# Down-projection in seven block products, with its left operands prepared in the up stage

## Chip, cores and metric

One core of one Trainium2 chip. The metric is the device time of one execution in microseconds, for the slowest core; here there is only one. All arithmetic is float32 at the interface; inside, each matmul operand is split into a high part (float32r) and a low remainder, and each product is three matmuls: high by high, high by low, low by high.

## The reference

One decoder layer of 1024 tokens and width 1024: a mixer (a state-space scan beside sparse attention), a LayerNorm, then the feed-forward part, then a second LayerNorm. The change lies in the feed-forward part and what follows it:

```
def _conv_ffn(h, w_up, conv_w, conv_b, w_down):
    u = _causal_dwconv(h @ w_up, conv_w, conv_b)
    gate, up = jnp.split(u, 2, axis=-1)
    return (jax.nn.silu(gate) * up) @ w_down
...
        h = _layer_norm(DEEPNORM_ALPHA * x + m, ln1_g[i], ln1_b[i])
        f = _conv_ffn(h, ffn_w_up[i], ffn_conv_w[i], ffn_conv_b[i], ffn_w_down[i])
        x = _layer_norm(DEEPNORM_ALPHA * h + f, ln2_g[i], ln2_b[i])
```

`w_up` is 1024 x 5632, the convolution has width 3 along the tokens, `w_down` is 2816 x 1024.

## The kernel before

The framework orders each engine's instructions by a priority list against a simulated clock, and gives out buffers from pools with fixed counts; only SyncE, which issues the loads, keeps the order of the program. Every engine then runs its list in order, so an instruction that waits holds those behind it.

**Up stage** (the loop over `j`, 22 tiles of 128 channels). For each `j`, two raw weight tiles are loaded (`up_load`), and `w_prep` forms four combinations on VectorE (lines 988 to 991), then seven operand pairs: a high copy on ScalarE (line 996) and a low remainder on GpSimd (line 997). TensorE runs seven block products (`product`, 12 matmuls each, 84 in all) in place of eight. They accumulate in PSUM banks `pa`, `pb`, `pc`, `pd`; VectorE and ScalarE combine them into `xg` and `xu` (lines 1023 to 1047). A bank is read between the two products that accumulate on it: `c1` must be copied out of `pa` (line 1023) while the next product runs on `pb`. Then comes the convolution: one ScalarE pass with scale and bias (line 1052) from SBUF to SBUF, two VectorE passes for the other taps (line 1055), for `xu` and `xg`, each 1024 wide; SiLU (line 1056), the product of the two (line 1057), and one store of 512 KB to DRAM (`g_dr`, line 1058), issued from ScalarE's queue.

**Down stage** (two halves of 512 tokens). For each half all eight PSUM banks accumulate, over 22 tiles `k` of the inner dimension. `prep(k)` loads a row tile of `w_down` (512 KB) and the half of `g_dr` (256 KB), and splits both: `w_hi` on ScalarE (line 129), `w_lo` on GpSimd (line 130), `g_hl` on ScalarE and VectorE (lines 1074 and 1075). `down(k, b)` is six matmuls. For the last three or four `k` of a half (`TAILS`) the loop over token tiles is outermost, so that the residual sum (line 1102) and `layer_norm` (lines 223, 224, 755, 756, 765, 766) of one token tile run beside the matmuls of the next.

All matmuls go through `three` (lines 157 to 159).

Of the kernel before, what the change touches and what calls it, by code (L numbers as in the profile page):

```python
# [15 lines left out]
P = 128  # L16
# [41 lines left out]
def hybrid_layer(ctx, tc, x, w_in, ssd_conv_w, ssd_conv_b, dt_bias, a_log, d_skip, ssd_norm_g,  # L58
# [14 lines left out]
    BUFS = {"wr": 3, "wh": 3, "wl": 3, "t4": 18, "wo": 8, "pp": 8, "pt": 3, "tx": 3}  # L73
# [48 lines left out]
    g_dr = dram.tile([DFF, L], F32, name="g_dr")  # L122
# [895 lines left out]
    def first(j, w):  # L1018

        a = bank("pa", "ip")  # L1020
        product(a, w[0], h11, True)
        c1 = mid("c1")
        nc.scalar.activation(c1, a, AF.Copy)
        return a, c1

    for j in range(NF):
        up_load(j + 1)
        w = ws.pop(j)
        a, c1 = first(j, w)
# [102 lines left out]
```

## Time and profile before

| | us |
|---|---|
| median of 3 runs | 1746.84 (1745.46 to 1746.99) |
| the profiled execution | 1747.83 |
| its span, first to last instruction | 1745.8 |
| up stage, dense part | 1075 to 1486.5 |
| TensorE idle between the stages | 1486.5 to 1494.4 |
| down stage | 1494.4 to 1736.8 |
| after the last matmul | 1736.8 to 1745.8 |

The profile is of one execution. A matmul's own duration overlaps with its neighbours', so its price in a dense stretch is the distance from one start to the next. A group's duration of VectorE or GpSimd includes the time in which the instruction was held by the other engine. The granted clock is a share of 2.4 GHz.

### The profile page before, as it was taken

The numbers are of one execution on the slowest core, as the hardware profiler recorded it, in microseconds if no ns is written. First come the engines' busy times: TensorE is split into PE (matmuls) and PEld (weight loads), VectorE is DVE, ScalarE is ACT, GpSimd is POOL, SyncE is SP. The second block draws the span as 40 slices with busy tenths as digits, with TensorE's granted clock in tenths as the row PEclk, the third lists the DMA queues.
The fourth block names the chain that finished last, engine by engine and source line by source line (L and its number), as shares of the span: only waits on it lengthen the run. The fifth ranks groups of instructions, "written<-read, shape, count | busy, mean of one in ns | idle before, by whom it ended". The sixth has DMA issues, their size and how long they took to land.

```text
span 1745.8 us, 22765 instructions
## 1 busy us (share of the span) xinstructions
PE 1624.8 (93%) x7976; PEld 1346.9 (77%) x7976; DVE 1192.9 (68%) x2089; ACT 889.3 (51%) x1625; POOL 801.3 (46%) x560
## 2 busy tenths in 40 slices
PE   7899998998998699999999977999999999899997
PEld 5688887776897568777787755888888888688886
DVE  3533779999368477787777478887887786515516
ACT  3333597687632476666666344544444443333231
POOL 2222234634265254545454348755555552445351
PEclk9999999999999889999999987999999999899999
DMA  5122022131333464454553551222222223446443
GB/s 168 38 79 67 27 92 88 43 115 52 125 103 91 151 202 127 127 167 118 162 147 124 171 169 60 85 94 76 77 84 93 85 73 115 139 145 229 157 153 125
DMA packets 180938, 198.22 MB, mean 114 GB/s; under 512 B 12003, under 2 KB 136279, under 8 KB 180823
## 3 DMA queue, kind: packets, MB, share of 16 engines
q1 hardware_dynamic: 147351, 145.37, 28.1%
q10 hardware_dynamic: 33472, 51.39, 8.1%
q8 instruction: 63, 1.03, 0.3%
q14 instruction: 52, 0.43, 0.1%
HBM read 145.28 MB, written 51.45 MB: 113 GB/s over the span
## 4 chain that ended last, share of the span: by engine, by line
PE 50%; DVE 8%; issue 2%; ACT 2%; DMA 2%; POOL 0%; ACTq 0%; DVEq 0%; POOLq 0%; SPq 0%
PE acc L157 5%; PE acc L159 5%; PE acc L158 5%; PE ops L157 3%; PE ops L158 3%; PE ops L159 3%; PE ptp L689 3%; PE pc L157 2%; PE pc L158 2%; PE pc L159 2%; PE pa L157 2%; PE pd L158 2%; PE pd L157 2%; PE pd L159 2%; PE pa L158 2%
## 5 line engine op out<-in xcount | busy, mean ns | idle before, releaser
L130 POOL TENSOR_TENSOR w_lo<-w_raw,w_hi 128x1024 fp32r<-128x1024 f32 (+1 forms) x89 | 222.0, 2500 | 162.5 <-ACT w_hi L129 160.3
L157 PE MATMUL proj<-xTh,w_hi 128*128 128x512 f32 (+1 forms) x432 | 174.1, 403 | 18.3 <-POOL w_hi L127 6.6
L159 PE MATMUL proj<-xTh,w_lo 128*128 128x512 f32 (+1 forms) x432 | 173.1, 402 | 2.8 <-POOL w_lo L130 2.8
L158 PE MATMUL proj<-xTl,w_hi 128*128 128x512 f32 (+1 forms) x432 | 174.6, 404 | 0.0
L997 POOL TENSOR_TENSOR w_hl<-s,w_hl 128x512 fp32r<-128x512 f32 x88 | 129.1, 1472 | 83.8 <-ACT w_hl L996 83.5
L683 POOL TENSOR_SCALAR prob<-prob,sm 128x512 f32<-128x512 f32 (+7 forms) x128 | 96.3, 763 | 139.7 <-DVE sm L682 109.9
L1075 DVE TENSOR_TENSOR g_hl<-g_raw,g_hl 128x512 fp32r<-128x512 f32 x44 | 62.0, 1422 | 131.4 <-ACT g_hl L1074 131.4
L997 POOL TENSOR_TENSOR w_hl<-w_raw,w_hl 128x512 fp32r<-128x512 f32 x66 | 105.4, 1599 | 88.3 <-ACT w_hl L996 57.9
L157 PE MATMUL acc<-w_hi,g_hl 128*128 128x512 f32 x352 | 136.3, 395 | 7.8 <-ACT g_hl L1074 7.8
L158 PE MATMUL acc<-w_lo,g_hl 128*128 128x512 f32 x352 | 137.7, 391 | 0.0
L159 PE MATMUL acc<-w_hi,g_hl 128*128 128x512 f32 x352 | 137.6, 391 | 0.0
L127 POOL TENSOR_SCALAR w_hi<-w_raw 128x1024 fp32r<-128x1024 f32 x35 | 40.0, 1143 | 172.1 <-PE proj L158 135.6
L680 ACT ACTIVATE prob<-prob,mx 128x512 f32<-128x512 f32 (+7 forms) x128 | 98.4, 771 | 35.9 <-DVE mx L677 35.7
L691 ACT ACTIVATE pt<-ptp 128x512 fp32r<-128x512 f32 x144 | 81.1, 594 | 64.3 <-PE ptp L689 43.7
L157 PEld LDWEIGHTS proj<-xTh,w_hi 128*128 128x128 f32 (+1 forms) x432 | 83.1, 192 | 37.9 <-issue 7.1
L157 PE MATMUL ops<-w_hi,y_hi 128*128 128x512 f32 x256 | 103.7, 405 | 3.1 <-ACT y_hi L129 3.1
L692 DVE TENSOR_TENSOR pt<-ptp,pt 128x512 fp32r<-128x512 f32 x144 | 95.5, 684 | 15.6 <-ACT pt L691 15.2
L158 PE MATMUL ops<-w_lo,y_hi 128*128 128x512 f32 x256 | 102.6, 401 | 0.4 <-DVE w_lo L130 0.4
L353 ACT ACTIVATE junk<-score,cand 128x1024 bf16<-128x1024 f32 (+2 forms) x96 | 85.9, 895 | 32.4 <-DVE cand L367 30.6
L129 ACT ACTIVATE w_hi<-w_raw 128x1024 fp32r<-128x1024 f32 (+1 forms) x62 | 65.1, 1052 | 72.8 <-PE acc L159 48.1
L159 PE MATMUL ops<-w_hi,y_lo 128*128 128x512 f32 x256 | 101.2, 398 | 0.0
L157 PE MATMUL tps<-w_hi,xTh 128*128 128x256 f32 x320 | 95.1, 298 | 3.6 <-ACT tout L611 2.1
(314 smaller groups left out, 4788.9 us busy)
## 6 DMA issues: line engine op xcount, KB each, us to landing
w_raw<-in_ffn_w_up_dram SPq DMA_DIRECT2D x44, 512.0 KB, 3.9
w_raw<-in_ffn_w_down_dram SPq DMA_DIRECT2D x44, 512.0 KB, 3.7
w_raw<-in_w_in_dram SPq DMA_DIRECT2D x36, 512.0 KB, 4.8
r_dr<-rout ACTq DMA_DIRECT2D x48, 256.0 KB, 2.1
g_dr<-vg ACTq DMA_DIRECT2D x22, 512.0 KB, 2.6
g_raw<-g_dr SPq DMA_DIRECT2D x44, 256.0 KB, 4.0
acsb<-a_dr SPq DMA_DIRECT2D x16, 512.0 KB, 4.0
w_raw<-in_w_out_dram SPq DMA_DIRECT2D x16, 512.0 KB, 4.6
```

The source lines that it names most:

```text
L129: nc.scalar.activation(hi, raw, AF.Copy)
L130: (nc.vector if lo_on_dve else nc.gpsimd).tensor_tensor(lo, raw, f(hi), op=OP.subtract)
L157: nc.tensor.matmul(ps, ah, bh, start=start, stop=False, skip_group_check=onto)
L158: nc.tensor.matmul(ps, ah, bl, start=False, stop=False, skip_group_check=onto)
L159: nc.tensor.matmul(ps, al, bh, start=False, stop=stop, skip_group_check=onto)
L353: nc.scalar.activation(junk[1][:, :n], score_ap[b], AF.Sign, bias=c, scale=-1.0, accum_out=val[e][:, i:i + 1])
L680: nc.scalar.activation(t[:, :w], t[:, :w], AF.Exp, bias=mx[:, h:h + 1], scale=-1.0, accum_out=sm[:, h:h + 1])
L683: nc.gpsimd.tensor_scalar(t[:, :w], t[:, :w], sm[:, 4 + h:5 + h], 1.0, op0=OP.mult, op1=OP.mult)
L691: nc.scalar.activation(pt[:, 0], ps, AF.Copy)
L692: nc.vector.tensor_tensor(pt[:, 1], ps, f(pt[:, 0]), op=OP.subtract)
L997: nc.gpsimd.tensor_tensor(t[:, 1], src, f(t[:, 0]), op=OP.subtract)
L1075: nc.vector.tensor_tensor(t[:, 1], raw, f(t[:, 0]), op=OP.subtract)
```

## The change

Down-projection: the tokens, the inner dimension and the output columns are each cut in two, and the eight block products of that cut become seven (a Strassen-Winograd scheme), named P1 to P7. Each is 11 tiles `k` by 4 token tiles by 3 matmuls, 512 columns wide. They run in the order P1, P2, P6, P7, P4, P5, P3 on two sets of four banks, `pa` and `pb`; P2, P4 and P3 accumulate on top of what the set already holds (`onto`), after VectorE or ScalarE has read it.

The left operands: three products take blocks of g as stored in `g_dr`, and split them in the down stage as before. The other four need q1, q2, q3 and a plain block. These are formed and split in the up stage, after every second `j`, and kept in DRAM as high and low parts (`gs_dr`). So that a pair of tiles from the two halves of the inner dimension is at hand together, the up loop visits the channel tiles in the order 0, 11, 1, 12, and so on (`pair_of`).

The convolution: it works on halves of 512 tokens, and the accumulating tile `v_` is a PSUM bank in place of an SBUF tile.

The right operands: 11 tiles of `w_down`'s blocks stay in SBUF (`keep`) and are changed in place from product to product; the others are loaded again. The second LayerNorm is cut up: the residual sums of one half of the tokens are made after P4 and P5, those of the other after P2 and P3, and `last_norm` ends each tile.

The diff, cut to its core:

```diff
-    BUFS = {"wr": 3, "wh": 3, "wl": 3, "t4": 18, "wo": 8, "pp": 8, "pt": 3, "tx": 3}
+    BUFS = {"wr": 3, "wh": 3, "wl": 3, "t4": 18, "wo": 8, "pp": 8, "pt": 3, "tx": 4}
...
+    g_dr = dram.tile([DFF // 2, 3, 512], F32, name="g_dr")
+    gs_dr = dram.tile([DFF // 2, 2, 4, 512], F32, name="gs_dr")
...
+    def conv_half(x_, tag, ct, half):
+        v_ = bank("v", tag)
+        o = half * 512
+        nc.scalar.activation(v_, x_[:, o:o + 512], AF.Identity, bias=fw[:, 132 + ct:133 + ct], scale=fw[:, 88 + ct:89 + ct])
+        for sft in (1, 2):
...
+            nc.vector.scalar_tensor_tensor(v_[:, z:], x_[:, o - sft + z:o + 512 - sft], tap, v_[:, z:],
+                                           op0=OP.mult, op1=OP.add)
...
+        now(nc.scalar.activation, c1, a, AF.Copy)
+        bb = bank("pb", "pv")
...
+        for half in range(2):
+            hs = slice(half * 512, half * 512 + 512)
+            vu = conv_half(xu, "lg", cu, half)
+            vg = conv_half(xg, ("ip", "tp")[half], cg, half)
+            nc.scalar.activation(gt[:, hs], vg, AF.Silu)
+            nc.vector.tensor_tensor(gt[:, hs], gt[:, hs], vu, op=OP.mult)
+        rows = slice(j // 2 * P, (j // 2 + 1) * P)
+        if j % 2 == 0:
+            v1 = gt
+            nc.scalar.dma_start(g_dr[rows, 0], v1[:, :512])
+        else:
+            lo1, hi1, lo2, hi2 = v1[:, :512], v1[:, 512:], gt[:, :512], gt[:, 512:]
+            nc.scalar.dma_start(g_dr[rows, 1], lo2)
+            q1, q2 = mid("q1", tag="ev"), mid("q2", tag="ev")
+            nc.vector.tensor_tensor(q1, hi1, hi2, op=OP.add)
+            nc.vector.tensor_tensor(q2, q1, lo1, op=OP.subtract)
+            q3, q4 = hi1, lo1
+            nc.gpsimd.tensor_tensor(q3, lo1, hi1, op=OP.subtract)
+            nc.gpsimd.tensor_tensor(q4, lo2, q2, op=OP.subtract)
+            nc.scalar.dma_start(g_dr[rows, 2], q4)
+            for n, (q, hi) in enumerate(((q1, xu[:, :512]), (q2, xu[:, 512:]), (q3, xg[:, :512]), (hi2, xg[:, 512:]))):
+                hi, lo = hi.bitcast(F32R), q.bitcast(F32R)
+                nc.scalar.activation(hi, q, AF.Copy)
+                nc.gpsimd.tensor_tensor(lo, q, f(hi), op=OP.subtract)
+                nc.scalar.dma_start(gs_dr[rows, 0, n], f(hi))
+                nc.scalar.dma_start(gs_dr[rows, 1, n], f(lo))
...
+        if p == "P6":
+            raw = w_two(p, k, KT, 512)
+            nc.vector.tensor_tensor(b2, raw, b2, op=OP.subtract)
+            nc.vector.tensor_tensor(b1, b2, b1, op=OP.add)
+            return b1
...
+        gt = big("g_hl", F32R, (P, 2, 512), "pp")
+        if p in RAW:
...
+            nc.scalar.activation(gt[:, 0], raw, AF.Copy)
+            nc.vector.tensor_tensor(gt[:, 1], raw, f(gt[:, 0]), op=OP.subtract)
+        else:
+            nc.sync.dma_start(f(gt), gs_dr[k * P:(k + 1) * P, :, PAIR[p]])
+        w_raw = right(p, k)
+        wt = big("wd_hl", F32R, (P, 2, 512), "t4" if p == "P3" else WDTAG[n_prep[0] % 2])
+        nc.scalar.activation(wt[:, 0], w_raw, AF.Copy)
+        nc.gpsimd.tensor_tensor(wt[:, 1], w_raw, f(wt[:, 0]), op=OP.subtract)
...
+    run("P1", pa, False)
+    for t in range(4):
+        now(nc.scalar.activation, c1[t], pa[t], AF.Copy)
+    r1 = h_rows(0)
+    run("P2", pa, True)
...
+    run("P4", pa, True)
+    for t in range(4):
+        nc.vector.scalar_tensor_tensor(r2[t][:, N1], r2[t][:, N1], ALPHA, u2[t], op0=OP.mult, op1=OP.add)
+        nc.vector.scalar_tensor_tensor(r1[t][:, N2], r1[t][:, N2], ALPHA, u2[t], op0=OP.mult, op1=OP.add)
+        nc.vector.scalar_tensor_tensor(r2[t][:, N2], r2[t][:, N2], ALPHA, u3[t], op0=OP.mult, op1=OP.add)
+        nc.vector.tensor_tensor(r2[t][:, N1], r2[t][:, N1], pa[t], op=OP.add)
+        stats(st8[4 + t], 0, r2[t])
+    run("P5", pb, False)
+    for t in range(4):
+        now(nc.vector.tensor_tensor, r2[t][:, N2], r2[t][:, N2], pb[t], op=OP.add)
+    for t in range(4):
+        last_norm(r2[t], st8[4 + t], 4 + t)
...
+    run("P3", pb, True, 6, finish_tile)
```

## Rows read from the trace of the kernel before

**Rows 1.** The page, part 1: busy us, share of the span, instructions per engine.
```profile
PE 1624.8 (93%) x7976; PEld 1346.9 (77%) x7976; DVE 1192.9 (68%) x2089; ACT 889.3 (51%) x1625; POOL 801.3 (46%) x560
```

**Rows 2.** Busy time by stretch; last columns: granted clock, DMA share, GB/s.
```profile
1075.00:1486.50 411.50, 410.20 (x1805) 338.09 (x1803) 323.28 (x299) 185.88 (x257) 223.48 (x150) 1.00 0.27 86
1486.50:1494.40 7.90, 0.06 (x2) 0.03 (x1) 6.26 (x7) 3.76 (x4) 0.52 (x1) 0.74 0.00 0
1494.40:1500.70 6.30, 6.30 (x15) 4.95 (x16) 6.30 (x3) 3.04 (x4) 6.30 (x3) 0.52 0.71 227
1500.70:1736.80 236.10, 236.10 (x1042) 195.20 (x1040) 95.35 (x111) 70.99 (x90) 102.97 (x42) 1.00 0.50 165
```

**Rows 3.** TensorE's waits from 1075 us on: releaser, total us, times, longest.
```profile
PE pc L157 <- DVE u L1040: 0.9, 1, 0.9
```

**Rows 4.** Timeline of TensorE in the down stage: start us, us, instruction.
```profile
1559.93 0.39 PE L157 MATMUL acc<-w_hi,g_hl 128*128 128x512 f32 x1
1560.16 0.39 PE L158 MATMUL acc<-w_lo,g_hl 128*128 128x512 f32 x1
```

**Rows 5.** Timeline of ScalarE at the change of stage.
```profile
1491.80 1.06 ACT L1056 ACTIVATE vg<-vg 128x1024 f32<-128x1024 f32 x1 [2.73 <-DVE vg L1055]
1492.76 1.04 ACT L129 ACTIVATE w_hi<-w_raw 128x1024 fp32r<-128x1024 f32 x1
```

**Rows 6.** Groups of the up stage, 1075 to 1494: busy us, mean ns, idle before.
```profile
L997 POOL TENSOR_TENSOR w_hl<-s,w_hl 128x512 fp32r<-128x512 f32 x84 | 122.8, 1466 | 78.6 <-ACT w_hl L996 78.4
L996 ACT ACTIVATE w_hl<-s 128x512 fp32r<-128x512 f32 x84 | 52.2, 625 | 50.6 <-PE pc L159 36.0 <-DVE s L990 4.2 <-PE pb L159 4.1
L1055 DVE SCALAR_TENSOR_TENSOR vu<-xu,fw,vu 128x1022 f32<-128x1022 f32 x22 | 40.7, 1849 | 0.0
L1057 DVE TENSOR_TENSOR vg<-vg,vu 128x1024 f32<-128x1024 f32 x22 | 32.4, 1473 | 3.0 <-ACT vg L1056 3.0
L1055 DVE SCALAR_TENSOR_TENSOR vu<-xu,fw,vu 128x1023 f32<-128x1023 f32 x22 | 28.5, 1296 | 26.1 <-ACT vu L1052 26.1
L1056 ACT ACTIVATE vg<-vg 128x1024 f32<-128x1024 f32 x22 | 23.4, 1062 | 43.2 <-DVE vg L1055 43.2
L1040 DVE TENSOR_TENSOR u<-u,pc 128x512 f32<-128x512 f32 x22 | 14.8, 674 | 0.4 <-PE pc L159 0.4
L1023 ACT ACTIVATE c<-pa 128x512 f32<-128x512 f32 x22 | 13.1, 594 | 20.3 <-PE pa L159 9.4 <-DVE vg L1057 6.5 <-PE pc L159 3.4
```

**Rows 7.** Timelines of VectorE and GpSimd in the up stage.
```profile
1286.61 1.79 DVE L988 TENSOR_TENSOR s<-w_raw 128x512 f32<-128x512 f32 x1
1288.32 0.68 DVE L990 TENSOR_TENSOR s<-w_raw 128x512 f32<-128x512 f32 x1
...
1286.09 1.76 POOL L997 TENSOR_TENSOR w_hl<-w_raw,w_hl 128x512 fp32r<-128x512 f32 x1 [1.79 <-ACT w_hl L996]
...
1300.11 1.30 POOL L997 TENSOR_TENSOR w_hl<-w_raw,w_hl 128x512 fp32r<-128x512 f32 x1 [1.42 <-ACT w_hl L996]
```

**Rows 8.** ScalarE's waits in the up stage: total us, times, longest.
```profile
ACT w_hl L996 <- DVE vg L1057: 39.4, 10, 4.0
```

**Rows 9.** Groups of the down stage, 1494 to 1746.
```profile
L1075 DVE TENSOR_TENSOR g_hl<-g_raw,g_hl 128x512 fp32r<-128x512 f32 x44 | 62.0, 1422 | 131.4 <-ACT g_hl L1074 131.4
L1102 DVE SCALAR_TENSOR_TENSOR r<-r,acc 128x512 f32<-128x512 f32 x16 | 10.8, 674 | 9.1 <-PE acc L159 9.1
```

**Rows 10.** Two stretches of 6 us in the down stage, columns as in the second group.
```profile
1590.00:1596.00 6.00, 6.00 (x29) 4.95 (x28) 4.72 (x2) 1.44 (x2) 4.17 (x2) 1.00 0.98 369
1632.00:1638.00 6.00, 6.00 (x28) 4.97 (x27) 1.02 (x1) 0.53 (x1) 3.27 (x2) 1.00 0.74 227
```

**Rows 11.** Timeline of VectorE after the last matmul.
```profile
1738.86 0.69 DVE L223 BATCH_NORM_STATS2 bnst<-r 128x6 f32<-128x512 f32 x1
...
1741.35 1.41 DVE L766 SCALAR_TENSOR_TENSOR r<-r,lnmv,ln_b 128x512 f32<-128x512 f32 x2
```

More of the change, by code (lines that the diff above doesn't have):

```diff
@@ L922, in hybrid_layer, with pair_of @@
     raws = {}
+    def pair_of(n):
+        return n // 2 + n % 2 * (NF // 2)
     def up_load(j):
@@ L1016, in product, with now @@
                   start and k == 0, k == 3, not start)
-    def first(j, w):
+    def now(call, *a, **k):
+        with tc.high_priority(EV_PRIO):
+            call(*a, **k)
+    def conv_half(x_, tag, ct, half):
[3 more added lines that the diff above has]
+        for sft in (1, 2):
+            tap = fw[:, (2 - sft) * 44 + ct:(2 - sft) * 44 + ct + 1]
+            z = 0 if half else sft
+            nc.vector.scalar_tensor_tensor(v_[:, z:], x_[:, o - sft + z:o + 512 - sft], tap, v_[:, z:],
+                                           op0=OP.mult, op1=OP.add)
+        return v_
+    for j in range(NF):
+        up_load(j + 1)
+        w = ws.pop(j)
         a = bank("pa", "ip")
@@ new lines, in h_rows, with mm, run @@
+    def h_rows(half):
+        out = []
+        for t in range(4):
+            r = big("r2", tag="wo")
+            nc.sync.dma_start(r, h_dr[(half * 4 + t) * P:(half * 4 + t + 1) * P, :])
+            out.append(r)
+        return out
+    def mm(ps, ops, t, first, last, onto):
+        gt, wt = ops
+        ts = slice(t * P, (t + 1) * P)
+        three(ps, gt[:, 0, ts], gt[:, 1, ts], wt[:, 0], wt[:, 1], first, last, onto)
+    def run(p, acc, onto, tail=0, done=None):
+        ops = []
+        for k in range(KT):
+            ops.append(prep(p, k))
+            if k < KT - tail:
+                for t in range(4):
+                    mm(acc[t], ops[k], t, k == 0 and not onto, k == KT - 1, onto)
+        for t in range(4):
+            for k in range(KT - tail, KT):
+                mm(acc[t], ops[k], t, False, k == KT - 1, onto)
+            if done:
+                done(t)
@@ new lines, in hybrid_layer @@
+    st8 = [small(f"st{b}", (P, 2, 6), bufs=1) for b in range(NB)]
+    run("P1", pa, False)
[3 more added lines that the diff above has]
+    run("P2", pa, True)
+    for t in range(4):
+        now(nc.vector.scalar_tensor_tensor, r1[t][:, N1], r1[t][:, N1], ALPHA, pa[t], op0=OP.mult, op1=OP.add)
+        stats(st8[t], 0, r1[t])
+    run("P6", pb, False)
+    for t in range(4):
+        now(nc.vector.tensor_tensor, u2[t], c1[t], pb[t], op=OP.add)
@@ new lines, in hybrid_layer @@
+    r2 = h_rows(1)
+    run("P7", pa, False)
+    for t in range(4):
+        now(nc.vector.tensor_tensor, u3[t], u2[t], pa[t], op=OP.add)
+    run("P4", pa, True)
+    for t in range(4):
+        nc.vector.scalar_tensor_tensor(r2[t][:, N1], r2[t][:, N1], ALPHA, u2[t], op0=OP.mult, op1=OP.add)
[3 more added lines that the diff above has]
+        stats(st8[4 + t], 0, r2[t])
```

155 lines of the change are left out of this document (82 added, 73 removed).

## The prediction

> **What bounds the kernel now.** The page's first part comes first: TensorE is busy 93% of the span, VectorE 68%, ScalarE 51%, GpSimd 46% [rows 1]. That is a mean over stages, so the table of stretches comes next [rows 2]. In the dense part of the up stage (411.5 us) and in the down stage from 1500.7 us on (236.1 us) TensorE has no gap and the granted clock is 1.00, its upper level. Between them lie 7.9 us without a matmul, and 6.3 us at a granted clock of 0.52, the lower level, in which only 15 matmuls start. After the last matmul come 9.0 us. TensorE's waits say the same: from 1075 us on the longest beside the gap is 0.9 us [rows 3]. So both stages are set by the count of matmuls, and what the other engines do is hidden as long as it keeps ahead.
>
> The price of a matmul is the distance between starts, not its 0.39 us: 1560.16 - 1559.93 [rows 4], or 236.1 us / 1042 = 0.2266 us [rows 2]. I use 0.2267 for a 128x512 matmul.
>
> **Part 1, fewer matmuls.** Before: 22 tiles x 8 token tiles x 2 halves of the columns x 3 = 1056. After: 7 x 11 x 4 x 3 = 924. 132 fewer x 0.2267 = -29.9 us. They lie on the path, since TensorE has no gap there.
>
> **Part 2, the change of stage.** The gap is 7.9 us, and the slow stretch costs 6.3 - 15 x 0.2267 = 2.9 us, together 10.8 [rows 2]. The cause stands in ScalarE's line: the first split of a weight tile (1492.76) sits behind the SiLU of the last `j` (1491.80), which waited 2.73 us for VectorE [rows 5]; TensorE starts only after it. After the change the first product takes all four banks of `ip` and `tp`, of which one holds the gate's second half of the last convolution. That is free after the last sum (0.67, line 1040), the scaling (0.59, as line 1023), two taps (0.67 each) and SiLU (about half of 1.06) [rows 6]: 3.1 us, with hand-overs about 4. Three banks are free earlier, and each step prepared ahead gives them 9 matmuls, 2 us, so this can be covered; or ScalarE's queue can again hold the first split back. Bounds of what is left: 0 to 10.8. I take 4.8, nearer to the bank's chain, thus -6.0.
>
> **Part 3, the up stage.** TensorE's work per `j` stays 84 x 0.2267 = 19.0 us. Per `j` the others do now, by rows 2 divided by 411.5 / 19.04 = 21.6: VectorE 15.0, ScalarE 8.6, GpSimd 10.3 us.
> - VectorE. Convolution and gating now cost 8.1 us per `j`: lines 1055 and 1057, of which two forms of four stand in [rows 6] at 1.85 and 1.30 us, with 1.47 for the product (the other two forms lie between them). After: eight half taps and two half products. They read one operand from PSUM, as line 1040 does at 0.67 us also while GpSimd works, so 6.7 us; q1 and q2 add, per `j`, 0.68 to 1.79 us [rows 7]. Sum 7.4 to 8.5: no change. If writing to PSUM brought no relief, each half would be 0.92 us and VectorE would reach some 18 of 19 us.
> - GpSimd gets six more operations per pair, three per `j`, at 1.30 to 1.76 us [rows 7]: 14 to 15.6 of 19 us. After an odd `j` they come in a lump of 8 to 11 us; the weights' low parts behind them have slack, since ten buffers of operands serve seven products, so a buffer's next use is nine products (24 us) away.
> - ScalarE gets 2 copies per `j` at 0.63, and 5.5 stores in place of one at about 0.33 each; the four half scalings cost what two whole ones did. Near 11.3 of 19 us. What matters is order: a store waits in ScalarE's queue for the engine that makes its data, and holds `c1`, which TensorE needs 12 matmuls (2.72 us) later. Today one store per `j` holds ScalarE up to 4.0 us, 39.4 us in ten waits [rows 8], and TensorE loses nothing. After there are seven such stores per pair.
> - The load order (`pair_of`) changes no count. DRAM traffic grows by 0.9 MB per `j`, 48 GB/s on 86; the down stage runs at 165 [rows 2].
> I take +2 us; bounds 0, and the second rival.
>
> **Part 4, feeding the down stage.** A step is 12 matmuls, 2.72 us. In it ScalarE makes one or two copies (0.63 each), GpSimd one low part (1.30 alone), VectorE one operation on two SBUF operands (0.68 alone), in P6 two, in P7 none. VectorE and GpSimd hold each other up there: 1.79 in place of 0.68 [rows 7], a mean of 1.42 for line 1075 [rows 9]. If such operations exclude each other fully, P6 needs 1.30 + 2 x 0.68 = 2.66 of 2.72 us and the others 2.0, so P6 just holds, and six buffers of right operands carry a lead into it.
> SyncE's queue: the load of a left operand waits for one of eight `pp` buffers, and behind it wait the loads of the right operands; so loads run up to eight steps (22 us) ahead. Issues number some 121 of about 0.4 us: no bound. Bytes per step: 0.79 MB in P2, P6, P4 and P5 (three tiles of 256 KB), 289 GB/s; less in the rest. The down stage now moves 165 GB/s, but 369 at a DMA share of 0.98 over 6 us [rows 10], made of the same transfers of 256 and 512 KB. So it fits, at about 0.8 of that peak. The Trainium skill speaks against it: "DMA: Bandwidth & Descriptors", Bandwidth, wants transfers of 1 MiB or more and gives 2.0 us + bytes / 436e3 for one; estimated from that, a 256 KB transfer alone would move 100 GB/s and a step would take over 7 us. The 369 GB/s disagrees, because several are in flight. I take +1 us for feeding, bounds 0 and the third rival.
> Seams: P2, P4 and P3 start on banks just read. A bank's last matmul lies 0.68 us before the next bank's, so the first has 2 us for a copy of 0.6. Each of three seams costs 0 to 1.5 us; +1 in all.
>
> **Part 5, the end.** After P5's last matmul VectorE has four sums (2.4 us), four norms, the low parts for P3 that aren't made yet, and for each token tile of P3 a sum and a norm. One norm takes 1738.86 to 1742.76, 3.9 us [rows 11]. With eight left operands prepared ahead, three low parts remain at about 1 us: 2.4 + 15.6 + 3 + 4 x 4.5 = 39.0, and 3.0 from the last norm to the end of the span: 42.0 us. TensorE needs 132 x 0.2267 = 29.9 for P3, plus today's 9.0: 38.9. So VectorE sets the end by about +3 us. With no lead at all, eleven low parts at 1.42 us [rows 9] give 54.6, which is +15.7. If the norms fill each other's waits: 0.
>
> **Sum.** -29.9 - 6.0 + 2 + 1 + 1 + 3 = -28.9. The profiled execution took 1747.8 us (span 1745.8 and 2.0 around it): 1718.9. It lay 1.0 above the median of the runs: 1718.
>
> **Rivals.**
> 1. VectorE bounds P5 and P3 (0.15). For it: after P4 twelve more operations on two SBUF operands and the norms of P5 fall together with P5's differences and P3's low parts, and GpSimd holds each of these up. Against it: the lead of eight steps. Time: +15.7 in place of +3, 1731.
> The Trainium skill bears on this: "SBUF — State Buffer", Who interferes with whom, says that a VectorE instruction with two SBUF inputs and a GpSimd instruction that reads SBUF exclude each other, and one with at most one SBUF input is free. By it the taps in PSUM cost 0.67 each and the norms collide; line 1102, with one operand in PSUM, has a mean of 0.67 and agrees [rows 9].
> 2. Stores hold ScalarE in the up stage, so that `c1` is late; this one is slower (0.10). A wait of 4.0 us ahead of `c1` costs 4.0 + 0.6 - 2.72 = 1.9 us. Two in each of 11 pairs cost 42 us in place of 2: 1758. From about 2.9 us per pair on the change loses (32 us). For it: seven stores where one waits up to 4.0 us [rows 8]. Against: today's waits cost TensorE nothing, and `c1` now has priority.
> 3. The DMA doesn't sustain its peak (0.05). At the 227 GB/s seen at a share of 0.74 [rows 10] 44 steps take 3.46 us in place of 2.72: +33, hence about 1750, within noise of no change or just slower.
> 4. The seam of the stages is covered and the end isn't late: 1718 - 4.8 - 3 - 2 = 1708 (0.08).
> That the count of matmuls doesn't fall can be left out; the loops fix it.
>
> **How the numbers follow.** Forecast 0.62, rivals 0.15, 0.10, 0.05 and 0.08. Range 1706 to 1737: forecast, rivals 1 and 4, with the open ends of parts 2 and 3. 0.2% (3.5 us) is about what a measurement of this kernel can tell from no change. Faster: 0.62 + 0.15 + 0.08 and a little of rivals 2 and 3 where they are mild, 0.86. Same: 0.03. Slower: the rest of 2 and 3, 0.11.
>
> **What would show it.** Right: 924 matmuls at 0.2267 us in the down stage with the clock at 1.00; a gap between the stages under 5 us; the up stage again 411 us from its dense start; taps at 0.67 us; some 12 us after the last matmul. Wrong: in the up stage TensorE waiting for ScalarE's `c1` with a store ahead of it; in P3 TensorE waiting for line-1075's successor behind the norms; in P2, P6, P4 or P5 a DMA share near 1 and waits for `w_down` or `gs_dr`.

## The result, and the profile after

| | before | changed |
|---|---|---|
| median, us | 1746.26 (1745.46 to 1746.99, 4 runs) | 1727.88 (1727.09 to 1730.53, 4 runs) |
| ratio | 1 | 0.9897 [0.9883, 0.9911] |
| profiled execution, us | 1747.83 | 1727.09 |
| span, us | 1745.8 | 1725.4 |

The change gains 18.4 us between the medians and 20.4 between the profiled spans; the forecast sum was 28.9. 1727.9 lies inside the range, 10 us above the predicted 1718.

To see where the difference went, I cut each trace at three matmul starts: the first of the up stage, the last of the up stage, the last of all. "Beyond the matmuls" is the stretch from the last up matmul to the last of all, less 0.2267 us for each down matmul: 1056 (239.4 us) before, 924 (209.5 us) after.

| us | first up matmul starts | up stage | last up matmul to last matmul | beyond the matmuls | last start to span's end |
|---|---|---|---|---|---|
| before | 1030.3 | 455.9 | 250.4 | 11.0 | 9.3 |
| changed | 1030.7 | 460.7 | 224.1 | 14.7 | 9.9 |
| difference | +0.4 | +4.8 | -26.2 | +3.7 | +0.6 |

-29.9 for the matmuls, +3.7, +4.8, +0.6 and +0.4 make the -20.4.

The table of stretches of the changed kernel answers [rows 2]. Columns: stretch, its length, busy us (and instructions) of TensorE's matmuls, weight loads, VectorE, ScalarE, GpSimd; granted clock, DMA share, GB/s.

```profile
1134.00:1142.00 8.00, 5.30 (x23) 3.73 (x21) 7.09 (x9) 3.46 (x6) 6.45 (x5) 1.00 0.29 98
1142.00:1491.60 349.60, 349.57 (x1541) 288.75 (x1539) 259.43 (x363) 186.74 (x305) 234.95 (x174) 1.00 0.41 136
1491.60:1498.10 6.50, 4.94 (x14) 3.45 (x14) 6.50 (x9) 5.31 (x11) 5.12 (x4) 0.74 0.12 9
1498.10:1511.70 13.60, 13.60 (x61) 11.05 (x59) 10.77 (x10) 5.67 (x11) 10.12 (x8) 1.00 0.92 319
1511.70:1519.80 8.10, 0.15 (x1) 0.00 (x0) 0.00 (x0) 0.65 (x2) 2.06 (x2) 0.70 1.05 410
1519.80:1526.50 6.70, 6.67 (x18) 5.30 (x19) 5.44 (x4) 5.81 (x11) 6.65 (x5) 0.59 0.73 253
1526.50:1715.75 189.25, 189.25 (x835) 156.32 (x834) 117.93 (x155) 56.07 (x96) 99.16 (x67) 1.00 0.73 246
```

Apart from 8 us near its start, the up stage is dense (349.57 of 349.6 us), and so is the down stage from 1526.5 us on: 835 matmuls in 189.25 us, 0.2266 each. What is lost in the down stage lies in the first 35 us of P1. The old gap between the stages (8.2 us from one matmul start to the next) has shrunk to 1.57 us; the first 6.5 us of P1, at a granted clock of 0.74, hold 14 matmuls and lose 3.3 us. Six steps later there is a new gap of 8.4 us from start to start (the stretch from 1511.7 us), in which all engines stand nearly still and the DMA is full. The granted clock, 1.00 ahead of that gap, is 0.59 behind it: 18 matmuls in 6.7 us, which loses 6.7 - 18 x 0.2267 = 2.6 us more. TensorE's waits from 1075 us on (releaser, total us, times, longest) name the one who was late, as [rows 3] did:

```profile
PE acc L158 <- ACT wd_hl L1157: 9.2, 2, 8.0
PE pd L158 <- DVE xg L1020: 1.6, 1, 1.6
PE pb L160 <- POOL w_hl L997: 1.1, 1, 1.1
PE acc L159 <- POOL wd_hl L1158: 0.4, 1, 0.4
```

It is ScalarE's split of a right operand (line 1157). ScalarE's timeline around the gap, where [rows 5] showed it before:

```profile
1507.29 2.07 ACTq L1086 DMA_DIRECT2D gs_dr<-xu  x2
1509.41 0.63 ACT L1084 ACTIVATE xg<-gt 128x512 fp32r<-128x512 f32 x1 [1.54 <-DMA keep<-in_ffn_w_down_dram]
1512.31 0.33 ACTq L1087 DMA_DIRECT2D gs_dr<-gt  x1
1513.11 0.33 ACTq L1086 DMA_DIRECT2D gs_dr<-xg  x1
1514.99 0.33 ACTq L1087 DMA_DIRECT2D gs_dr<-q  x1
1518.72 0.33 ACTq L1081 DMA_DIRECT2D g_dr<-gt  x1
1519.15 0.63 ACT L1157 ACTIVATE wd_hl<-keep 128x512 fp32r<-128x512 f32 x1 [9.11 <-DMA keep<-in_ffn_w_down_dram]
```

Between 1510.0 and 1519.15 us ScalarE computes nothing and only issues four stores of the last pair, one by one. The split that TensorE needs stands behind them. Its own data was long there, although the row names that load: SyncE had issued it 22 us earlier (1497.01), and the load's semaphore was complete at 1502.17. SyncE's timeline:

```profile
1497.01 1.09 SPq L1111 DMA_DIRECT2D keep<-in_ffn_w_down_dram  x2
...
1503.90 2.62 SPq L1165 DMA_DIRECT2D r<-h_dr  x4
```

(The first row is the loads of `keep` for steps 6 and 7, the second the four loads of `r1`.)

What holds the stores is told by the program's own instruction list for ScalarE. Each DMA signals its landing on one of eight semaphores, given out in turn to the loads of SyncE and the stores of ScalarE alike. Where an earlier DMA on the same semaphore may still be under way, the list makes the issue wait for its landing.

```
L1084 ACTIVATE xg<-gt          waits GpSimd
L1087 DMA gs_dr<-gt            waits DMA semaphore 4, GpSimd
L1086 DMA gs_dr<-xg            waits DMA semaphore 6, ScalarE
L1087 DMA gs_dr<-q1            waits DMA semaphore 0, GpSimd
L1081 DMA g_dr<-gt             waits DMA semaphore 1, GpSimd
L1157 ACTIVATE wd_hl<-keep     waits DMA semaphore 3, TensorE     (step 6 of P1, counted from 0)
L1157 ACTIVATE wd_hl<-keep     waits DMA semaphore 5, TensorE     (step 7)
```

So a store waits for whatever DMA had the semaphore last, and the split waits for the store. By the times at which the trace shows these semaphores complete, the first of the four stores waited for a load of `r1` (until 1512.23) and the fourth for a load of P2 (1518.64); the second and third waited for ScalarE's own earlier stores (1513.03 and 1514.92). All these DMAs were slow: the four loads of 512 KB for `r1` needed 6.6 to 9.8 us from issue to landing.

### The profile page after: what moved, and what is told of

It is laid out like the page before. It is cut to its first block, busy times and chain, and to the rows that moved or that the text cites. A ratio compares the mean times of both kernels' runs of the same rounds, so it can differ in the third digit from the quotient of the medians.

```text
span 1725.4 us, 23252 instructions
## 1 busy us (share of the span) xinstructions
PE 1598.4 (93%) x7844; PEld 1322.7 (77%) x7844; DVE 1212.8 (70%) x2274; ACT 921.4 (53%) x1761; POOL 873.9 (51%) x659
## 4 chain that ended last, share of the span: by engine, by line
PE 52%; DVE 6%; DMA 2%; ACT 2%; issue 1%; POOL 1%; ACTq 0%; DVEq 0%; SPq 0%; POOLq 0%
PE acc L158 4%; PE acc L159 4%; PE acc L160 4%; PE ops L158 3%; PE ops L159 3%; PE ops L160 3%; PE ptp L690 3%; PE pa L158 2%; PE pa L160 2%; PE pa L159 2%; PE pc L160 2%; PE pc L158 2%; PE pc L159 2%; PE pd L158 2%; PE pd L160 2%; PE pd L159 2%
## 5 line engine op out<-in xcount | busy, mean ns | idle before, releaser
L997 POOL TENSOR_TENSOR w_hl<-s,w_hl 128x512 fp32r<-128x512 f32 x88 | 120.0, 1371 | 58.2 <-ACT w_hl L996 54.2
L131 POOL TENSOR_TENSOR w_lo<-w_raw,w_hi 128x1024 fp32r<-128x1024 f32 (+1 forms) x45 | 113.3, 2521 | 26.1 <-ACT w_hi L130 23.9
L159 PE MATMUL acc<-wd_hl,g_hl 128*128 128x512 f32 x308 | 121.1, 395 | 0.4 <-POOL wd_hl L1158 0.4
L160 PE MATMUL acc<-wd_hl,g_hl 128*128 128x512 f32 x308 | 120.9, 394 | 0.0
L997 POOL TENSOR_TENSOR w_hl<-w_raw,w_hl 128x512 fp32r<-128x512 f32 x66 | 91.0, 1381 | 58.7 <-ACT w_hl L996 56.6
L158 PE MATMUL acc<-wd_hl,g_hl 128*128 128x512 f32 x308 | 110.9, 395 | 9.2 <-ACT wd_hl L1157 9.2
L1158 POOL TENSOR_TENSOR wd_hl<-keep,wd_hl 128x512 fp32r<-128x512 f32 x55 | 82.5, 1526 | 53.5 <-ACT wd_hl L1157 47.0
L160 PEld LDWEIGHTS proj<-xTh,w_lo 128*128 128x128 f32 (+1 forms) x432 | 82.7, 192 | 20.0 <-POOL w_lo L131 3.2
```

The costliest lines, as they stand in the source:

```text
L131: (nc.vector if lo_on_dve else nc.gpsimd).tensor_tensor(lo, raw, f(hi), op=OP.subtract)
L158: nc.tensor.matmul(ps, ah, bh, start=start, stop=False, skip_group_check=onto)
L159: nc.tensor.matmul(ps, ah, bl, start=False, stop=False, skip_group_check=onto)
L160: nc.tensor.matmul(ps, al, bh, start=False, stop=stop, skip_group_check=onto)
L997: nc.gpsimd.tensor_tensor(t[:, 1], src, f(t[:, 0]), op=OP.subtract)
L1158: nc.gpsimd.tensor_tensor(wt[:, 1], w_raw, f(wt[:, 0]), op=OP.subtract)
```

## Experiments

All times below are medians, with the ratio to the kernel before and its interval; the stage figures come from one trace each, cut as above. The time at which the up stage starts lay between 1026.7 and 1036.0 us in the 14 traces, though no edit touches what runs ahead of it. So stages are compared rather than whole spans, and a difference of some 3 us between medians isn't read.

| run | median, us | ratio | up stage | last up to last matmul | beyond the matmuls |
|---|---|---|---|---|---|
| changed kernel | 1727.88 | 0.9897 [0.9883, 0.9911] | 460.7 | 224.1 | 14.7 |
| e1 r1 late | 1726.22 | 0.9885 [0.9862, 0.9908] | 461.5 | 220.0 | 10.5 |
| e2 stores from GpSimd | 1727.88 | 0.9895 [0.9871, 0.9919] | 464.6 | 220.7 | 11.2 |
| e3 old buffer order | 1717.57 | 0.9839 [0.9813, 0.9864] | 457.2 | 216.5 | 7.1 |
| e4 no splits, no `gs_dr` stores | 1715.95 | 0.9831 [0.9806, 0.9856] | 459.1 | 212.6 | 3.2 |
| e5 P1's splits first | 1722.90 | 0.9873 [0.9843, 0.9903] | 463.0 | 219.9 | 10.4 |
| e6 convolution alone | 1741.92 | 0.9977 [0.9962, 0.9993] | 458.3 | 241.4 | 2.0 |
| e7 old order, r1 late | 1717.80 | 0.9849 [0.9822, 0.9877] | 456.5 | 216.6 | 7.1 |
| e8 the same, splits first | 1716.58 | 0.9839 [0.9814, 0.9864] | 458.1 | 215.8 | 6.4 |
| e9 stores from SyncE | 1730.41 | 0.9916 [0.9895, 0.9937] | 461.3 | 226.1 | 16.6 |
| e10 old order, stores from SyncE | 1720.74 | 0.9866 [0.9843, 0.9889] | 457.0 | 223.9 | 14.4 |
| e11 stores and r1 put off | 1721.67 | 0.9865 [0.9847, 0.9883] | 461.1 | 220.1 | 10.6 |
| e12 old order, both put off | 1716.82 | 0.9829 [0.9813, 0.9845] | 457.8 | 215.9 | 6.5 |

### e1: r1's loads later

```diff
-    r1 = h_rows(0)
-    run("P2", pa, True)
+    r1 = []
+    run("P2", pa, True, load=lambda: r1.extend(h_rows(0)))   # called at k == 8
```

> The four 512 KB loads of r1 (needed only after P2) are issued at step 8 of P2 instead of ahead of P2; nothing else changes. In the changed kernel TensorE waits 7.98 us for ScalarE's split of a right operand (1511.7 to 1519.8) with the DMA at a share of 1.05 and 410 GB/s, then runs 6.7 us at a granted clock of 0.59 (18 matmuls, 2.6 us lost). Theory A: the 2 MB of r1 fill the DMA there, so the last pair's stores and the loads of P1's right operands land late; without them the wait at 1511.7 falls to under 2 us, the slow clock behind it goes, and the time falls by 6 to 10.6 us (to 1717 to 1722). Theory B: the right operands' loads are issued too late whatever else is in flight; wait and time stay (within 2 us). Theory C: the last pair's stores in ScalarE's queue hold its splits whatever the DMA carries; the wait stays within 2 us too.

The gap falls from 8.4 to 3.9 us, a stretch at a low granted clock remains behind it, and the stage is 4.1 us shorter. So `r1`'s loads are a part of the cause, about half, and not the whole: theory A is too large. Whether they do it by filling the DMA or by holding a semaphore that a store waits for, this run doesn't tell: without them the DMA's share in the shorter gap is still 0.97 (1514.9 to 1518.8 us). Theory B is out without this run, since the split's data had landed 17 us before it.

### e2: the last pair's stores from GpSimd

```diff
-                nc.scalar.dma_start(gs_dr[rows, 0, n], f(hi))
-                nc.scalar.dma_start(gs_dr[rows, 1, n], f(lo))
+                eng = nc.gpsimd if j == NF - 1 else nc.scalar
+                eng.dma_start(gs_dr[rows, 0, n], f(hi))
+                eng.dma_start(gs_dr[rows, 1, n], f(lo))
```

> The eight stores of the split left operands of the last pair are issued from GpSimd instead of ScalarE; r1 stays where it is. Theory C: these stores stand in ScalarE's queue ahead of P1's splits and wait there; moved away, the 8 us wait in P1 falls below 3 us and the time falls by 5 to 10 us. Theory A: the DMA is full, so P1's right operands land as late as before, and the wait stays between 5 and 9 us; the time within 3 us. Against both: GpSimd now holds its own low parts of the weights behind the issue of the stores, which could add up to 8 x 1 us there.

TensorE's longest wait in P1 is now for GpSimd (total us, times, longest):

```profile
PE acc L159 <- POOL wd_hl L1159: 4.6, 2, 4.2
```

VectorE's timeline shows six low parts of left operands that take 16 us, which one by one are 3.81, 1.75, 5.54 and three of about 1.77 us:

```profile
1512.01 16.04 DVE L1153 TENSOR_TENSOR g_hl<-raw,g_hl 128x512 fp32r<-128x512 f32 x6 [0.55 <-ACT g_hl L1152]
```

The wait has moved to the queue that now carries the stores. The down stage is 3.4 us shorter; the up stage was 3.8 us longer in this trace, 1.9 of it at a single wait for VectorE that e5 shows as well, and the time is unchanged. Neither C (below 3 us) nor A (5 to 9 us) foresaw this size.

### e3: the old order of the weights' buffers

```diff
-    WTAG = ("wh", "wl", "wh", "wl", "pp", "pp", "wh", "wl", "pp", "pp")
+    WTAG = ("wh", "wl", "pp", "wh", "wl", "pp", "wh", "wl", "pp", "pp")
```

> Only the order in which the up stage's weights take their operand buffers is put back to that of the kernel before. Theory: the changed order made the second j's weight sums come ahead of the low parts of t2 on VectorE, which TensorE waits 6.2 us for (3.97 before); with the old order the wait at the start of the up stage falls back to about 4 us and the up stage ends 2 to 3 us earlier; time -2.4 us. Rival: the start of the up stage is set by other work (ScalarE's high parts of t2), so the wait stays and the time stays within 1 us; or the old order holds GpSimd's low parts back later in the stage, and the time rises.

This one line is worth 10 us: 3.5 in the up stage, a little more than expected, and 7.6 in the down stage, which neither theory foresaw. The line sets only when operand buffers come free, but the instruction lists are made against a simulated clock, and they come out differently. In the up stage the two waits at 1134 to 1142 us are gone (1.6 and 1.1 us), and VectorE takes the low parts of `t2` ahead of the next weights' sums. In the changed kernel these came first; there the dense part begins 39.3 us after the stage's first start, in e3 36.6, in the kernel before 37.9. VectorE's timeline of the changed kernel:

```profile
1061.64 1.22 DVE L988 TENSOR_TENSOR s<-w_raw 128x512 f32<-128x512 f32 x1
1062.78 1.22 DVE L990 TENSOR_TENSOR s<-w_raw 128x512 f32<-128x512 f32 x1
...
1066.87 1.63 DVE L989 TENSOR_TENSOR s<-s,w_raw 128x512 f32<-128x512 f32 x1
1068.42 2.35 DVE L913 TENSOR_TENSOR t2l<-t2raw,t2h 128x256 fp32r<-128x256 f32 x2
```

In P1, ScalarE's timeline of e3 has the splits of steps 6 and 7 ahead of six of the eight stores, of which six had stood ahead of them:

```profile
1506.06 0.61 ACT L1157 ACTIVATE wd_hl<-keep 128x512 fp32r<-128x512 f32 x1
1506.58 0.61 ACT L1151 ACTIVATE g_hl<-raw 128x512 fp32r<-128x512 f32 x1
1507.10 0.61 ACT L1157 ACTIVATE wd_hl<-keep 128x512 fp32r<-128x512 f32 x1
1507.26 0.33 ACTq L1086 DMA_DIRECT2D gs_dr<-xu  x1
...
1514.77 0.33 ACTq L1081 DMA_DIRECT2D g_dr<-gt  x1
1515.14 0.63 ACT L1157 ACTIVATE wd_hl<-keep 128x512 fp32r<-128x512 f32 x1 [6.91 <-DMA raw<-g_dr]
```

ScalarE is held nearly as long as before (6.91 us), but by then TensorE has two more steps to work on, 5.4 us. Its longest wait in P1 is now 1.5 us, and not for ScalarE but for GpSimd's low part:

```profile
PE acc L159 <- POOL wd_hl L1158: 1.9, 2, 1.5
```

The DMA is no less full here than in the changed kernel; the stretch from 1506.5 us, columns as above:

```profile
1506.50:1532.50 26.00, 24.52 (x108) 19.98 (x108) 9.99 (x11) 13.53 (x26) 20.17 (x15) 1.00 1.05 402
```

TensorE starts 108 matmuls in these 26 us, so a full DMA alone doesn't stop it. P1 itself gives back 8.7 us; 1.3 are lost again in the first step of P4, where TensorE waits for ScalarE's split and this for VectorE's difference (line 1130). The changed kernel's trace loses nothing there; e1, e2, e5 and e7 to e11 lose 0.6 to 2.1 us. Whether it is the splits' place in the list or the buffers themselves that helps P1, e5 is to tell.

### e4: without the splits and their stores

```diff
-            for n, (q, hi) in enumerate(((q1, xu[:, :512]), (q2, xu[:, 512:]), (q3, xg[:, :512]), (hi2, xg[:, 512:]))):
...
-                nc.scalar.dma_start(gs_dr[rows, 0, n], f(hi))
-                nc.scalar.dma_start(gs_dr[rows, 1, n], f(lo))
...
-            nc.sync.dma_start(f(gt), gs_dr[k * P:(k + 1) * P, :, PAIR[p]])
+            nc.sync.dma_start(f(gt), g_dr[k * P:(k + 1) * P, 0:2])
```

> Leaves out, in the up stage, the splitting of the four left operands and their stores to DRAM (per pair 4 copies on ScalarE, 4 low parts on GpSimd, 8 stores); P4 to P7 load the same number of bytes from columns of g_dr that hold other values. It prices this work. If it is hidden in the up stage as forecast: that stage shortens by no more than the 2.7 us lost once at 1134 to 1142; the rest of the gain is at the change of stage, where eight stores fewer stand in ScalarE's queue: by theory C the 8 us wait goes (time -8 to -13 us in all), by theory A it halves at most, since 2 MB of r1 stay and 2 MB of stores go (time -3 to -8 us), by theory B it stays (time -2 to -4 us).

This leaves out work that the result needs, so it only prices it. Without it 3.2 us are lost in the down stage in place of 14.7. So with these lists 11.5 us of the change of stage belong to the last pair's splits and stores (with the old order of buffers, e3, the loss beside them is 7.1 and not 14.7); in the up stage, where ten other pairs have the same work, it costs 1.6 us. The time falls by 11.9, within the 8 to 13 of theory C.

### e5: P1's splits first

```diff
+        pr = now if p == "P1" else (lambda call, *x, **y: call(*x, **y))
...
-        nc.scalar.activation(wt[:, 0], w_raw, AF.Copy)
-        nc.gpsimd.tensor_tensor(wt[:, 1], w_raw, f(wt[:, 0]), op=OP.subtract)
+        pr(nc.scalar.activation, wt[:, 0], w_raw, AF.Copy)
+        pr(nc.gpsimd.tensor_tensor, wt[:, 1], w_raw, f(wt[:, 0]), op=OP.subtract)
```

> Only the splits of the first block product (P1) get the priority that the evictions have; the order of the weights' buffers stays that of the changed kernel. In ScalarE's queue this puts the splits of P1's steps 6 and 7 ahead of five of the last pair's stores, behind which they stood. Theory D: what cost the change of stage is this place in the queue (a store there waits until a load, sometimes one of r1's 512 KB, has landed), and the old order of the buffers helped only because it moved the same two splits ahead of stores. Then the way from the last matmul of the up stage to the last matmul, 224.1 us in the changed kernel, falls to 215 to 219, and the time by 5 to 9 us; the up stage keeps its 460.7. Rival E: the order of the buffers itself matters (the last products of the up stage hold the buffers that the splits write); then it stays within 2 us of 224.

With the buffers' order unchanged, the 8.4 us gap is down to 1.0 us. So the place in the list made that gap. But the stage gives back only 4.3 us: the last stores now hold ScalarE at the end of P1, where the banks have to be copied out for P2, and 4.1 us are lost there.

TensorE's wait there:

```profile
PE acc L158 <- ACT cu L1020: 2.3, 1, 2.3
```

And ScalarE's timeline ahead of it:

```profile
1526.56 0.33 ACTq L1087 DMA_DIRECT2D gs_dr<-q  x1
1530.92 0.33 ACTq L1087 DMA_DIRECT2D gs_dr<-gt  x1
1531.29 1.15 ACT L1146 ACTIVATE g_hl<-raw 128x512 fp32r<-128x512 f32 x2 [7.81 <-DMA gs_dr<-q]
```

Here the priority moved the hold behind another instruction; it didn't take it away.

### e6: the convolution part alone

```diff
-    g_dr = dram.tile([DFF // 2, 3, 512], F32, name="g_dr")
-    gs_dr = dram.tile([DFF // 2, 2, 4, 512], F32, name="gs_dr")
+    g_dr = dram.tile([DFF, L], F32, name="g_dr")
...
-        rows = slice(j // 2 * P, (j // 2 + 1) * P)
...
+        nc.scalar.dma_start(g_dr[j * P:(j + 1) * P, :], gt)
```

Behind it stands the down-projection of the kernel before.

> The convolution accumulated in PSUM, with the changed up stage's banks, priorities and weight buffers, but whole g stored once per j and the down-projection of the kernel before. It prices the convolution part. Forecast: VectorE's load per j is unchanged (8.1 us before, 6.0 to 6.7 for eight half taps and two half products), TensorE's is unchanged, so the up stage is neither faster nor slower in its dense part; time within 4 us of before (1743 to 1751). Theory that the new buffer order costs: up stage +2 to +4 us, and with no stores of splits at the change of stage nothing more there. If the convolution itself cost time: over 1752. If it gains: the last SiLU comes earlier, so the gap at the change of stage shrinks from 8.2 to some 4 us: 1740 to 1744.

At the change of stage 2.0 us are lost in place of 11.0: the distance between the last up and the first down start is 1.5 us (8.2 before). That is a gain of 9.0 us, where the prediction's chain over the bank of the last convolution was priced at 6.0. The up stage is 2.4 us longer, 2.3 of it at its start (40.2 us to the dense part, 37.9 before), where its weights take the buffers in the changed kernel's order; it has none of the waits at 1134 us. From there on TensorE never waits, so the convolution itself costs nothing. Together -6.6; the median fell by 3.3, from 1745.2 in the runs beside it, and the trace's up stage started 4.1 us later than that of before.

### e7 and e8: the old order with r1 late, and with P1's splits first

Both combine edits shown above.

> The old order of the weights' buffers and r1's loads at step 8 of P2 together. Alone these gave 1717.6 and 1726.2 against 1727.9. With the old order the way from the last up matmul to the last matmul is 216.5 us, of which 209.5 are matmuls: 1.57 and about 2.5 us of waits, and some 3 us of slow clock at the start. r1's loads matter only for the wait of 2.3 us in P1: if they cause it, 214 us and a time of 1715; if not, 216.5 and 1717.5.

> The old order of buffers, r1's loads at step 8 of P2 and the priority for P1's splits. If the place in ScalarE's queue and the full DMA are all that is left of the waits in P1, no wait over 1 us remains after the first 12 matmuls and the way from the last up matmul to the last is 212 to 214 us (209.5 of matmuls, 1.3 of the first wait, 1 to 3 of the slow clock): 1713 to 1715 us. If something else holds P1 (VectorE's low parts, GpSimd's), it stays at 216 and 1717.

With the old order, r1's loads make no difference (216.6 against 216.5 us). With the splits first as well it is 215.8, and TensorE's waits for GpSimd add up to 2.8 us, so e8's second reading holds: with the splits ahead of the stores and r1 late, something else holds P1. e1's 4 us and e3's 7.6 us don't add.

### e9 and e10: the last pair's stores from SyncE

```diff
+    def store_late(eng):
+        while late:
+            eng.dma_start(*late.pop(0))
...
-                nc.scalar.dma_start(gs_dr[rows, 0, n], f(hi))
-                nc.scalar.dma_start(gs_dr[rows, 1, n], f(lo))
+                late.append((gs_dr[rows, 0, n], f(hi)))
+                late.append((gs_dr[rows, 1, n], f(lo)))
+                if j < NF - 1:
+                    store_late(nc.scalar)
...
+    store_late(nc.sync)
     r1 = h_rows(0)
```

> The eight stores of the last pair's splits are issued by SyncE, behind all loads of P1, instead of by ScalarE; the order of the weights' buffers is that of the changed kernel, r1's loads stay ahead of P2, and the same bytes move. ScalarE's queue then holds one store in P1. Theory D (stores that wait in ScalarE's queue hold the splits, and at the end of P1 the copies of its banks): the way from the last up matmul to the last matmul falls from 224.1 (and from 219.9 with the splits put first) to 211 to 214 us, time 1715 to 1718. Theory A (the DMA is full, and the loads land late whoever issues the stores): the wait moves to the landing of P1's right operands and 220 to 224 us remain.

> The same, with the old order of the weights' buffers, which alone gave 457.2 us for the up stage and 216.5 for the rest. Theory D: 457 + 211 to 214, so 1711 to 1714 us, faster than either part alone. Theory A: 216 stays, 1717.

Neither gains on its parent: the way to the last matmul is 2.0 us longer in e9 and 7.4 in e10. Theory D in its strong form, that clearing ScalarE's queue is enough, has fallen. The first gap shrinks as it should, from 8.4 to 2.8 us in e9 and from 1.9 to 0.6 in e10, but a second one of 4.9 and 6.7 us opens at the start of P2. SyncE's timeline in e10:

```profile
1502.54 0.41 SPq L1038 DMA_DIRECT2D gs_dr<-xu  x1
1509.72 0.32 SPq L1038 DMA_DIRECT2D gs_dr<-q  x1
...
1512.15 2.33 SPq L1173 DMA_DIRECT2D r<-h_dr  x4
1514.58 0.51 SPq L1107 DMA_DIRECT2D raw<-g_dr  x1
```

Its waits (total us, times, longest):

```profile
SPq L1038 <- POOL q L1091: 10.3, 2, 6.7
```

And the stretch from 1500 to 1508 us, columns as above:

```profile
1500.00:1508.00 8.00, 7.78 (x35) 6.12 (x34) 3.56 (x3) 5.04 (x10) 8.00 (x6) 1.00 0.26 99
```

SyncE waits for a low part that GpSimd hasn't made, the DMA runs nearly empty (share 0.26), and P2's first load goes out at 1514.6 us, behind eight stores and 2 MB of `r1`. Theory A, that the DMA is simply full, doesn't explain this either.

### e11 and e12: stores and r1 put off

The stores and r1's loads go to SyncE at step 8 of P2, behind P2's first loads.

```diff
-    r1 = h_rows(0)
-    run("P2", pa, True)
+    r1 = []
+    def later():
+        store_late(nc.sync)
+        r1.extend(h_rows(0))
+    run("P2", pa, True, load=later)   # called at k == 8
```

> The last pair's eight stores and r1's four loads are issued by SyncE at step 8 of P2, when the loads of P1 and of P2's first eight steps stand ahead of them; the buffers' order is that of the changed kernel. Issued by SyncE right behind P1's loads, the stores held P2's loads (SyncE waited 10.3 us for GpSimd's low parts, the DMA fell to a share of 0.26) and TensorE lost 4.7 and 6.5 us at the start of P2. Theory E: these stores aren't ready when their turn comes (GpSimd makes their data some 10 to 25 us after the last up matmul), so they hold whatever stands behind them in an in-order queue: ScalarE's splits, GpSimd's low parts or SyncE's loads. With nothing needed soon behind them, no wait over 1.5 us remains after P1's first 12 matmuls, and the way from the last up matmul to the last matmul is 211 to 215 us (224.1 in the changed kernel); time 1715 to 1719. Rival: the splits of the last pair hold GpSimd (eight operations of 1.3 to 1.7 us) and so P1's low parts, whoever stores; then some 4 us of waits for GpSimd remain and 216 to 218 us.

> The same with the old order of the weights' buffers (457 us for the up stage in three runs). Theory E: 457 + 211 to 214, time 1711 to 1715 us, the fastest of all. Rival: 216 and 1717, as with the old order alone.

Now no store holds a queue for more than 1.3 us, no gap opens at P2, and the rival is what remains: GpSimd. In e11 it makes five of its six operations on the last pair in one piece, and no low part of P1 for 9.0 us (1501.07 to 1510.12); TensorE runs out of steps and waits 3.1 us for it. GpSimd's timeline in e11:

```profile
1499.77 1.30 POOL L1166 TENSOR_TENSOR wd_hl<-keep,wd_hl 128x512 fp32r<-128x512 f32 x1 [2.45 <-ACT wd_hl L1165]
1501.70 1.67 POOL L1085 TENSOR_TENSOR gt<-gt 128x512 f32<-128x512 f32 x1 [0.63 <-DVE q L1082]
...
1508.44 1.72 POOL L1091 TENSOR_TENSOR gt<-gt,xg 128x512 fp32r<-128x512 f32 x1
1510.12 5.08 POOL L1166 TENSOR_TENSOR wd_hl<-keep,wd_hl 128x512 fp32r<-128x512 f32 x3
```

TensorE's wait for it:

```profile
PE acc L159 <- POOL wd_hl L1166: 3.5, 2, 3.1
```

In e12 GpSimd makes six low parts of P1 in a row first, then four operations of the last pair, and then alternates; the longest wait in P1 is 1.6 us. The old order of buffers thus still gives 4.2 us with the stores gone from both, 1.0 of them in the first step of P4. Its lists differ on all three engines, and which of the differences gives these 4.2 us wasn't separated.

**Which is best.** e3, e7, e8 and e12 lie at 1716.6 to 1717.8, not to be told apart. The old buffer order alone, e3, beats the changed kernel by 10.3 us and the kernel before by 1.6%; the other edits add nothing on top that these runs can measure.

## Why the prediction was right in sign and short in size

1727.9 lies in the range, but not for the reasons given for the range. Part 2's own bound was 10.8 us lost, and 14.7 were. The range reached past 1724 by rival 1, which did not occur, and by the open end of part 3; that it covers the last pair's work is luck.

**Part 1, the matmuls (-29.9): right.** 132 fewer at 0.2266, all on the path.

**Part 2, the change of stage (-6.0 forecast, +3.7 measured): this step failed.** The chain that it priced was even better covered than assumed: by e6, ahead of the old down-projection, it gives -9.0. The prediction named ScalarE's queue as what could hold the first split back, but gave it no price of its own. What it left out is that the last pair's splits and stores have no up stage left to hide in. Part 3 counted them as a lump beside 19 us of TensorE work per `j`; for the last pair that lump falls into P1, on ScalarE, GpSimd and the queues that P1 itself needs. e4 puts it at 11.5 us: -9.0 + 11.5 is +2.5, against the +3.7 of the traces; the other 1.2 us aren't assigned. With the same work and the old order of buffers 7.6 us less are lost (e3 against the changed kernel), so most of this price looks to be the order in which the lists take the work.

**Part 3, the up stage (+2 forecast, +4.8 measured).** None of the engines' loads came out higher than read. Per `j`, from the stretch 1142 to 1491.6 (18.4 times 19.04 us), VectorE has 14.1 us, ScalarE 10.2 and GpSimd 12.8; forecast were 15.0 without change, 11.3, and 14 to 15.6. The taps took 0.75 us where I took 0.67, with means of 0.744 to 0.754 in all their forms and 0.757 for the longest of the 176, beside a GpSimd that was busy two thirds of the time; [rows 6] had means of 1.30 to 1.85 for twice the width. Groups of the up stage, 1075 to 1486 us (busy us, mean ns, idle before):

```profile
L1030 DVE SCALAR_TENSOR_TENSOR v<-xu,fw,v 128x512 f32<-128x512 f32 x42 | 31.5, 751 | 0.0
L1067 DVE TENSOR_TENSOR gt<-gt,v 128x512 f32<-128x512 f32 x42 | 28.4, 677 | 0.0
L1026 ACT ACTIVATE v<-xg,fw 128x512 f32<-128x512 f32 x43 | 33.4, 778 | 18.3 <-DVE xg L1020 14.6 <-POOL q L1085 2.1 <-DVE v L1030 1.5
```

The Trainium skill, "SBUF — State Buffer", Who interferes with whom, lets a VectorE instruction with at most one SBUF input run beside GpSimd unhindered; the first two rows agree. The third row is the scaling, 0.78 us where I took 0.59 from a plain copy: the kernel before has the same operation at twice the width, at 1.247 us (line 1052), and that was the row to use. What was missed is the changed order of buffers, a line that the forecast didn't weigh and that moved the lists: the start takes 39.3 us in place of 37.9, and the two waits at 1134 to 1142 us cost 3.0 from start to start. The six traces with the new order and the splits have an up stage of 460.7 to 464.6 us, the five with the old order 456.5 to 458.1. With the old order the term is +0.6 to +2.2, as forecast.

**Part 4, feeding and seams (+2 forecast, 0 measured in the steady part).** From 1526.5 us on nothing waits; 246 GB/s at a share of 0.73. The three seams cost nothing. The formula that the prediction quotes from the Trainium skill, "DMA: Bandwidth & Descriptors", stands there under Anatomy of one DMA and is a fit for DMAs that GpSimd issues; the loads here are SyncE's. But the rate was judged as a mean over steps, and the burst at the start was not priced: in it P1's loads, P2's loads ahead of time, 2 MB of `r1` and the last stores come together, at 319 and 410 GB/s from 1498 to 1520 us.

**Part 5, the end (+3 forecast, +0.6 measured): mis-sized.** VectorE's timeline:

```profile
1683.99 0.69 DVE L1020 TENSOR_TENSOR r<-r,acc 128x512 f32<-128x512 f32 x1 [1.92 <-PE acc L160]
...
1704.39 0.69 DVE L1239 TENSOR_TENSOR r<-r,acc 128x512 f32<-128x512 f32 x1 [1.40 <-PE acc L160]
...
1712.09 0.67 DVE L1239 TENSOR_TENSOR r<-r,acc 128x512 f32<-128x512 f32 x1
...
1716.37 0.67 DVE L1239 TENSOR_TENSOR r<-r,acc 128x512 f32<-128x512 f32 x1
```

The first of P5's four sums starts before P5's last matmul, since the banks finish one after the other, and sums, norms and low parts are done by 1703 us, so VectorE waits 1.4 us for TensorE. A tile of P3 then costs it 4.3 us (1716.37 - 1712.09), where I took 4.5, against 6 x 3 x 0.2267 = 4.1 for TensorE's last steps. The last sum starts as the norm of the tile before ends (line 1205, 1716.38), half a microsecond after the last matmul (1715.91); that is about the 0.6 us.

**The rivals.** Rival 1 (VectorE bounds P5 and P3) did not occur: no TensorE wait there. Rival 2 had the right mechanism in the wrong place: `c1` is never late in the up stage, but stores in ScalarE's queue held the splits in P1. Rival 3 (a DMA that falls short of its peak) did not occur: where it was full it moved 410 GB/s. Rival 4, 1708, was reached by none of the runs.

The sum then: 9.7 us short in part 2 and 2.8 in part 3, 2.4 and 2 better in parts 5 and 4, and 0.4 in the start of the up stage: 8.5 of the 28.9.

**What stays open.** Which of the three engines' lists makes the 4.2 us between e11 and e12. Whether the two waits at 1134 to 1142 us come from GpSimd's or ScalarE's list: they are in all six traces with the new order and the splits, and in none with the old order or without the splits (e4 has one of 1.0 us, some 40 us later). What the last pair's work costs with the old order of buffers: e4 was run with the new one only. And why two of VectorE's operations take 3.8 and 5.5 us in e2.

## What to carry to other kernels

Work that is hidden in a loop has a last iteration: ask where its stores, copies and sums land once the loop is over, and whose queue they stand in. A store in an in-order queue holds whatever is behind it, until its data is made and until the DMA before it on its semaphore has landed; moving it to another queue only changed who was held here (with the new order of buffers TensorE's longest wait was 8.0 us by ScalarE, 4.2 by GpSimd, 4.5 by way of SyncE), unless nothing behind it was needed soon. And where a planner makes the instruction lists, read them for lines that look neutral: one tuple of buffer tags was worth 10 of 29 us here.

## What the runs showed of the hardware

- The DMA moved 410 GB/s for 8 us with transfers of 256 and 512 KB only, above the 369 of [rows 10], and e3 402 GB/s over 26 us. A 512 KB load of `r1` then took 6.6 to 9.8 us to land, where the weights' loads of 512 KB in the up stage have a median of 3.9. The Trainium skill, "DMA: Bandwidth & Descriptors", Bandwidth, asks for 1 MiB or more per transfer to reach 75% of the peak; with several in flight, half and a quarter of that gave 410 here.
- With stores issued from GpSimd (0.56 to 0.75 us each on its timeline), two of six VectorE operations of line 1153, on two SBUF operands of 128x512, took 3.81 and 5.54 us and four 1.75 to 1.78. Such an operation takes 0.68 or 1.79 in [rows 7]; in the kernel before's down stage the longest (line 1075) took 3.94.
